# Memory gates formed by rows and turned through DRAM, in a four-layer decoder trunk

## The chip, the core and the metric

One core of a Trainium2 chip runs the whole program. The metric is the device time of one execution in microseconds: before the change 2497.29 us, the median of three runs (2496.13, 2497.29 and 2500.47). TensorE (PE) multiplies, VectorE (DVE) and ScalarE (ACT) work on its results, GpSimd (POOL) here mostly issues DMAs, and SyncE (SP) issues the loads of the weights.

## The reference

Four layers, each with one input projection and one output projection, over 256 tokens of width 2048 in float32. Layers 0 and 3 mix tokens by latent attention, layer 1 by sparse attention, layer 2 by a sliding window; each layer also has four memory heads of width 256. Cut to what matters here:

```python
for i in range(DEPTH):
    h = _rmsnorm(x, norm_in[i])
    self_out, mq, gate = <mixer>(h, w_in, ...)        # h @ w_in, split
    mem_out = _memory_attention(mq, mem_n @ w_mem_kv[i])
    y = jnp.concatenate([self_out, mem_out], axis=-1) * jax.nn.silu(gate)
    x = x + y @ w_out[i]
return _rmsnorm(x, final_norm)
```

The gate has 3072 columns: 2048 for the self heads and 1024 for the memory heads. The norm's factor of each token (`rstd`) is not multiplied into `h` but into each product of it. With z = rstd * product / 2, SiLU of the gate is (tanh(z) + 1) * z.

## The kernel before, in words

**Products.** Each float32 operand is split in two parts, `hi` rounded to the matmul's format (ScalarE) and `lo` = value - `hi` (VectorE), and a product is hi*hi + hi*lo + lo*hi. Weights are loaded by SP into `wr` (five buffers) and split into `wh` and `wl` (`parts_of`, three buffers each). `split_in_order` chains these splits, so that they run in the order in which they are written. There are two forms of product. `rows_by` keeps 128 tokens of the activations in the array and moves 512 weight columns: three matmuls of 512 columns for each 128 rows of the weight (a k-tile) and each of two token tiles; the result has tokens on the partitions. `columns_by` keeps 128 weight columns in the array and moves the tokens' `hi` and `lo` side by side (512 columns) under `wh`, and `hi` alone (256 columns) under `wl`: for a k-tile of 256 weight columns two matmuls of 512 and two of 256 columns; the result has features on the partitions and the tokens along the free axis, in two sums that are added afterwards.

**Layers.** The gate and the output are worked off in six parts of 512 columns, in the order 4, 0, 1, 2, 3, 5: parts 4 and 5 belong to the memory heads, 0 to 3 to the self heads. A part projects its queries, issues its scores and softmax (`memory_attend`, `attend`), forms its gate, and leaves a list `steps`: `parts(0)`, `summed(0)`, `parts(1)`, `summed(1)`. `parts` splits the turned probabilities, `summed` multiplies them with the values (matmuls into `mo` or `o`) and ends in `gated` or `paired`, which multiply the sum with the gate `gT` and split the result into `y`. Then `w_out` multiplies the `y` of the part before (`pending`) with its rows of the output weight, in four chunks of 512 columns, and adds them to `x`. `rows_of_two` makes the first two chunks together.

**Two ways to a gate.** `gated` needs the gate with features on the partitions. Parts 0 to 3 use `gate_by_rows`: product by rows; ScalarE scales each row by its factor (a column of 128 values, `halves`) and takes the tanh; VectorE forms (tanh + 1) * z and transposes it in blocks of 32 x 32; POOL stores each token tile to DRAM and, when both have landed, fetches it back in four DMAs in the turned order. Parts 4 and 5 use `gate`: product by columns in two halves of 256 columns; `total` adds the two sums; VectorE multiplies by `nm.half`, in which the tokens' factors lie along the free axis and are the same on all partitions; tanh and the last step write `gT` in SBUF. `nm.half` is made once for each layer by `spread` (lines 179 to 185): two diagonal matrices, multiplied by ones.

**Order.** Each engine works through its own queue in order. A planner with modelled times sets that order when the program is built, by readiness and written order. `keep_in_program_order` pins an instruction to the written order, and `issue_after` puts one behind another on its engine. `hooks` are lists of functions that a product calls behind the given k-tile, which sets their place in the written order.

**Around the end of a layer.** After part 5's gate (lines 1382 to 1387) come chunks 0 and 1 of the pending part 3, part 5's sums, chunk 2 of the pending part, chunks 0 and 1 of part 5 itself, chunk 3 of the pending part, and chunks 2 and 3 of part 5. In the last layer (lines 1374 to 1381) part 5's own product comes after all four chunks of the pending one. In latent layers the steps of parts 4 and 0 to 3 are called as soon as the part's gate and the pending `w_out` are written (lines 1370 to 1373).

Of the kernel before, what the change touches and what calls it, by code (L numbers as in the profile page):

```python
# [15 lines left out]
P = 128  # L16
S = 256
# [16 lines left out]
def kernel(ctx: ExitStack, tc: tile.TileContext, a: dict, out: bass.AP,  # L34
# [141 lines left out]
            y = y2  # L176


    def spread(dst, cols):
        pr = misc("spr")  # L180
        for t in range(2):
            dg = wk.tile([P, S], F32, name="dg", tag="e", bufs=4)[:, :P]
            nc.vector.tensor_scalar(dg, ident, cols[:, t:t + 1], None, op0=OP.mult)
            nc.tensor.matmul(pr[:, t * P:(t + 1) * P], ones, dg, start=True, stop=True)
        nc.vector.tensor_copy(dst, pr[:, :S])


    def square_sum(col, src):
        junk = tmp("junk")
        return nc.scalar.activation(junk[:, :src.shape[-1]], src, AF.Square, accum_out=col)  # L190
# [166 lines left out]
                f()  # L357
        return acc if apart else whole

    def total(acc):  # L360
        z = wk.tile([P, 2, S], F32, name="z", tag="z", bufs=2)
        copy_act(z, acc[:, :, 1, :])
        nc.vector.tensor_add(z, z, acc[:, :, 0, :])
        return z

    def head_parts(dst, acc):

        z = wk.tile([P, 2, S], F32, name="zl", tag="z", bufs=2)
# [14 lines left out]
    class Norm:  # L383
# [38 lines left out]
        def finish(self):  # L422
            s2 = small("xs2", 2)
            nc.vector.tensor_reduce(s2, self.ss.rearrange("p (t c) -> p t c", t=2), AX.X, OP.add)
            self.rstd = small("xr", 2, bufs=3)
            rsqrt_mean(self.rstd, s2, D)
            self.eighth = small("x8", 2, bufs=3)
            nc.vector.tensor_scalar(self.eighth, self.rstd, 0.125, None, op0=OP.mult)
            half = self.halves = small("xh", 2, bufs=3)
            nc.vector.tensor_scalar(half, self.rstd, 0.5, None, op0=OP.mult)  # L430
            self.half = wk.tile([P, S], F32, name="half", tag="half", bufs=1)
            spread(self.half, half)

        def col(self, which, t):
            return getattr(self, which)[:, t:t + 1]
# [144 lines left out]
            copy_act(dst(i0, i1), f32(tp)[:, :(i1 - i0) * n].rearrange("p (j c) -> p j c", c=n)[:, :, 64 * late:])  # L580


    def gate(nm, w, c0, hooks):
        gT = None
        for h in range(2):
            z = total(columns_by(nm.at, 16, w, 0, (c0 + h * S, S), "g", hooks[h]))
            if gT is None:
                gT = act.tile([P, 4, S], F32, name="gT", tag="gT", bufs=1)
            nc.vector.tensor_mul(z, z, nm.half[:, None, :].to_broadcast([P, 2, S]))
            th = gT[:, 2 * h:2 * h + 2, :]  # L590
            nc.scalar.activation(th, z, AF.Tanh)
            nc.vector.scalar_tensor_tensor(th, th, 1.0, z, op0=OP.add, op1=OP.mult)
        return gT


    def gate_by_rows(nm, w, c0, hooks={}, between={}):
        acc = rows_by(nm.at, 16, w, 0, (c0, 512), "gr", hooks, None, between)
        gT = act.tile([P, 8, 4, 32], F32, name="gTr", tag="gT", bufs=1)
# [16 lines left out]

    def gated(y, o, gT, j):
        yt = wk.tile([P, 512], F32, name="yt", tag="yt", bufs=1)
        if gT.shape[1] == 8:
            nc.vector.tensor_mul(yt.rearrange("p (a t b) -> p a t b", a=2, b=32),
                                 o.rearrange("p (a t b) -> p a t b", a=2, b=32),  # L620
                                 gT[:, :, j:j + 2, :].rearrange("p t a b -> p a t b"))
        else:
            nc.vector.tensor_mul(yt, o, gT[:, j:j + 2, :].rearrange("p a b -> p (a b)"))
        y3 = yt.rearrange("p (a b) -> p a b", a=2)
        split(y[:, 0, j:j + 2, :], y[:, 1, j:j + 2, :], y3)

# [119 lines left out]
    def memory_project(nm, i, w, mq0, g0, part, steps, deferred, loaded=None, begun=None):  # L746
        qT, kT = [], []
        raw, v = loaded or memory_loads(i, part)

        def keys():  # L750
            hi = act.tile([P, 1024], F32R, name="mkh", tag="pq", bufs=PQ)
            tc.keep_in_program_order(copy_act(hi, f32(raw)))
            nc.vector.tensor_sub(raw, f32(raw), f32(hi))
            kT.extend(z.rearrange("p (t m b) -> p t m b", m=4, b=32) for z in (hi[:], raw[:]))
        for h in range(2):
            if part == 0:
                hooks = ({}, {4: [] if begun is not None else steps[:1]})[h]
            elif deferred:
                hooks = ({}, {4: steps[:1], 8: steps[1:2]})[h]
            else:  # L760
                hooks = ({0: steps[:1], 8: steps[1:3]}, {0: steps[3:]})[h]
            if h:
                hooks[8] = hooks.get(8, []) + [keys]
            acc = begun if h == 0 and begun is not None else columns_by(
                nm.at, 16, w, 0, (mq0 + part * 512 + h * 256, 256), "mq", hooks)
            q = act.tile([P, 2, 2, S], F32R, name="mqT", tag="pq", bufs=PQ)
            head_parts(q, acc)
            qT.append(q)
        if begun is not None:
            hooks = {4: steps}, {}  # L770
        elif deferred:
            hooks = {}, {0: steps[2:3], 4: steps[3:]}
        else:
            hooks = {8: [] if part else steps[1:]}, {}
        return (nm, kT, v, qT), lambda: gate(nm, w, g0 + 2048 + part * 512, hooks)

    def memory_attend(nm, kT, v, qT):
        ws = []
# [548 lines left out]
    for i in range(depth):  # L1327
# [22 lines left out]
        for part in (4, 0, 1, 2, 3, 5):  # L1350
# [16 lines left out]
            if part != 5:  # L1367
                if pending is not None:
                    w_out(*pending, False)
                if kind == 0:  # L1370
                    for f in steps:
                        f()
                    steps = []
# [75 lines left out]
```

## Time and profile before

| | us |
|---|---|
| time, median of three runs | 2497.29 |
| time of the profiled execution | 2496.1 |
| its span | 2494.3 |
| TensorE busy | 2483.5 (100%) |
| VectorE busy | 1806.1 (72%) |
| ScalarE busy | 1427.7 (57%) |
| GpSimd busy | 400.8 (16%) |

The span runs from the first to the last instruction. PE is the matmuls; PEld, the loading of the array, overlaps them. A busy TensorE says little, since matmuls overlap each other in the records: the distance of two starts tells what a matmul takes. The tiles of the two gates are `acc_g` (by columns) and `acc_gr` (by rows).

### The profile page before, as it was taken

How to read it: one execution, taken by the hardware profiler on the slowest of the kernel's cores; microseconds unless marked ns; L12 is line 12 of the kernel's file. 1: busy time of each engine (PE TensorE's matmuls, PEld its weight loads, DVE VectorE, ACT ScalarE, POOL GpSimd, SP SyncE). 2: the span in 40 equal slices, each digit the busy share in tenths (PEclk: the TensorE clock that was granted, in tenths of full speed). 3: DMA queues.
4: the chain of work that ended last, by engine and by line, in shares of the span. 5: the costliest groups of instructions: out<-in, count | busy, mean ns of one | idle time of the engine just before them, and what ended most of it. 6: DMA issues, size and time to landing. Idle time of an engine off the chain costs nothing.

```text
span 2494.3 us, 36407 instructions
## 1 busy us (share of the span) xinstructions
PE 2483.5 (100%) x12452; PEld 2109.9 (85%) x12452; DVE 1806.1 (72%) x3061; ACT 1427.7 (57%) x2278; POOL 400.8 (16%) x639
## 2 busy tenths in 40 slices
PE   9999999999999999999999999999999999999998
PEld 7888888888888888888888888888888888888887
DVE  6555655777677676878888775888887677767677
ACT  6444545555555556656666564666665655555554
POOL 1101011211120110112232101212220112012010
PEclk9999999999999999999999999999999999999999
DMA  9888887977877768689999697999978797788774
GB/s 311 279 292 284 283 281 221 260 208 214 220 226 219 217 221 243 193 268 271 264 284 262 197 285 217 283 270 271 270 223 252 232 251 217 198 220 241 239 210 147
DMA packets 462281, 607.59 MB, mean 244 GB/s; under 512 B 79536, under 2 KB 278976, under 8 KB 460944
## 3 DMA queue, kind: packets, MB, share of 16 engines
q1 hardware_dynamic: 420704, 476.92, 63.9%
q0 software_dynamic: 40672, 127.43, 17.3%
q8 instruction: 98, 1.61, 0.3%
q10 hardware_dynamic: 720, 0.93, 0.1%
q14 instruction: 87, 0.71, 0.1%
HBM read 541.49 MB, written 76.25 MB: 248 GB/s over the span
## 4 chain that ended last, share of the span: by engine, by line
PE 98%; DVE 1%; DMA 1%; ACT 0%; SPq 0%; issue 0%; DVEq 0%; ACTq 0%
PE acc_gr L329 5%; PE acc_gr L330 5%; PE acc_gr L328 5%; PE acc_g L352 5%; PE acc_mq L352 4%; PE acc_wo L328 4%; PE acc_wo L329 4%; PE acc_wo L330 4%; PE acc_qn L352 4%; PE acc_wo L243 3%; PE acc_wo L241 3%; PE acc_wo L242 3%; PE acc_q L329 2%; PE acc_q L330 2%; PE acc_q L328 2%; PE acc_mk L329 2%
## 5 line engine op out<-in xcount | busy, mean ns | idle before, releaser
L73 DVE TENSOR_TENSOR wl<-wr,wh 128x1024 fp32r<-128x1024 f32 (+2 forms) x860 | 1028.1, 1197 | 513.3 <-ACT wh L59 506.7
L59 ACT ACTIVATE wh<-wr 128x1024 fp32r<-128x1024 f32 (+2 forms) x860 | 891.3, 1038 | 811.0 <-PE acc_gr L330 96.9
L330 PE MATMUL acc_gr<-wh,xT 128*128 128x512 f32 x512 | 199.7, 390 | 0.0
L329 PE MATMUL acc_gr<-wl,xT 128*128 128x512 f32 x512 | 199.6, 390 | 0.0
L328 PE MATMUL acc_gr<-wh,xT 128*128 128x512 f32 x512 | 199.6, 390 | 0.0
L328 PE MATMUL acc_wo<-wh,y 128*128 128x512 f32 x432 | 168.3, 390 | 0.0
L330 PE MATMUL acc_wo<-wh,y 128*128 128x512 f32 x432 | 168.3, 390 | 0.0
L329 PE MATMUL acc_wo<-wl,y 128*128 128x512 f32 x432 | 168.3, 389 | 0.0
L352 PE MATMUL acc_g<-xT,wh 128*128 128x512 f32 x512 | 162.5, 395 | 0.0
L664 POOL DMA_DIRECT2D pL<-turn x192 | 120.2, 633 | 207.8 <-DMA turn<-T 111.5
L352 PE MATMUL acc_mq<-xT,wh 128*128 128x512 f32 x480 | 152.0, 396 | 0.0
L243 PE MATMUL acc_wo<-wh,y 128*128 128x512 f32 x320 | 124.9, 390 | 0.2 <-DVE y L63 0.2
L241 PE MATMUL acc_wo<-wh,y 128*128 128x512 f32 x320 | 124.9, 390 | 0.0
L242 PE MATMUL acc_wo<-wl,y 128*128 128x512 f32 x320 | 124.8, 390 | 0.0
L1346 DVE TENSOR_TENSOR x<-x,acc_wo 128x1024 f32<-128x1024 f32 x92 | 111.7, 1214 | 13.5 <-PE acc_wo L330 9.5
L352 PE MATMUL acc_qn<-cT,wh 128*128 128x512 f32 x384 | 121.3, 396 | 0.0
L354 PEld LDWEIGHTS acc_g<-xT,wl 128*128 128x128 f32 x512 | 95.6, 188 | 22.2 <-DVE wl L73 0.9
L330 PEld LDWEIGHTS acc_gr<-wh,xT 128*128 128x128 f32 x512 | 96.1, 188 | 19.6
L329 PEld LDWEIGHTS acc_gr<-wl,xT 128*128 128x128 f32 x512 | 96.1, 188 | 18.6
L328 PEld LDWEIGHTS acc_gr<-wh,xT 128*128 128x128 f32 x512 | 96.1, 188 | 18.6
L354 PEld LDWEIGHTS acc_mq<-xT,wl 128*128 128x128 f32 x480 | 89.0, 188 | 19.3
L354 PE MATMUL acc_g<-xT,wl 128*128 128x256 f32 x512 | 102.1, 279 | 0.1
(375 smaller groups left out, 5664.7 us busy)
## 6 DMA issues: line engine op xcount, KB each, us to landing
wr<-in_w_out_dram SPq DMA_DIRECT2D x192, 512.0 KB, 4.9
wr<-in_w_in_a_dram SPq DMA_DIRECT2D x176, 512.0 KB, 4.7
wr<-in_w_mem_kv_dram SPq DMA_DIRECT2D x126, 512.0 KB, 6.3
wr<-in_w_in_b_dram SPq DMA_DIRECT2D x116, 512.0 KB, 4.9
wr<-in_w_in_c_dram SPq DMA_DIRECT2D x104, 512.0 KB, 5.1
wr<-in_w_uq_dram SPq DMA_DIRECT2D x192, 128.0 KB, 3.5
turn<-T POOLq DMA_DIRECT2D x40, 384.0 KB, 5.1
tab<-flat POOLq DMA_DIRECT2D x8, 1536.0 KB, 11.5
```

The lines of the kernel that those rows point to most:

```text
L59: return nc.scalar.activation(o, i, AF.Copy, scale=scale)
L73: two = nc.vector.tensor_sub(lo, src, f32(hi))
L241: nc.tensor.matmul(accs[c][:, t], xh, wh[:, at], start=first, stop=False)
L242: nc.tensor.matmul(accs[c][:, t], xh, wl[:, at], start=False, stop=False)
L243: nc.tensor.matmul(accs[c][:, t], xl, wh[:, at], start=False, stop=last)
L328: nc.tensor.matmul(acc[:, t, :n], xh, wh[:, at], start=first, stop=False)
L329: nc.tensor.matmul(acc[:, t, :n], xh, wl[:, at], start=False, stop=False)
L330: nc.tensor.matmul(acc[:, t, :n], xl, wh[:, at], start=False, stop=last)
L352: nc.tensor.matmul(acc[j], wh[:, at[j]], q[:, :, kt % 4, :], start=first, stop=False)
L354: nc.tensor.matmul(acc[j][:, 0, :], wl[:, at[j]], q[:, 0, kt % 4, :], start=False, stop=last)
L664: nc.gpsimd.dma_start(f32(self.raw)[j * 32:(j + 1) * 32, :].rearrange("p (i r) -> p i r", r=r), bass.AP(tensor=d.tensor, offset=d.offset + ...
L1346: nc.vector.tensor_add(xs, xs, acc)
```

## The change

`gate`, `total` and `spread` go, and with them `nm.half`. The memory parts call `gate_by_rows`, and `gated` keeps the one form that reads its layout. The hooks of the gate's product are renumbered from two half products of four k-tiles a step to one product of two k-tiles a step, at about the same share of the work. In latent layers the steps of part 4 are no longer called at once: they are handed to `project(0)`, whose first product, of the rotary queries, takes them as hooks behind its k-tiles 0, 4 and 8.

```diff
-    def spread(dst, cols):
-        pr = misc("spr")
-        for t in range(2):
-            dg = wk.tile([P, S], F32, name="dg", tag="e", bufs=4)[:, :P]
-            nc.vector.tensor_scalar(dg, ident, cols[:, t:t + 1], None, op0=OP.mult)
-            nc.tensor.matmul(pr[:, t * P:(t + 1) * P], ones, dg, start=True, stop=True)
-        nc.vector.tensor_copy(dst, pr[:, :S])
...
-    def total(acc):
-        z = wk.tile([P, 2, S], F32, name="z", tag="z", bufs=2)
-        copy_act(z, acc[:, :, 1, :])
-        nc.vector.tensor_add(z, z, acc[:, :, 0, :])
-        return z
...
             nc.vector.tensor_scalar(half, self.rstd, 0.5, None, op0=OP.mult)
-            self.half = wk.tile([P, S], F32, name="half", tag="half", bufs=1)
-            spread(self.half, half)
...
-    def gate(nm, w, c0, hooks):
-        gT = None
-        for h in range(2):
-            z = total(columns_by(nm.at, 16, w, 0, (c0 + h * S, S), "g", hooks[h]))
-            if gT is None:
-                gT = act.tile([P, 4, S], F32, name="gT", tag="gT", bufs=1)
-            nc.vector.tensor_mul(z, z, nm.half[:, None, :].to_broadcast([P, 2, S]))
-            th = gT[:, 2 * h:2 * h + 2, :]
-            nc.scalar.activation(th, z, AF.Tanh)
-            nc.vector.scalar_tensor_tensor(th, th, 1.0, z, op0=OP.add, op1=OP.mult)
-        return gT
...
     def gated(y, o, gT, j):
         yt = wk.tile([P, 512], F32, name="yt", tag="yt", bufs=1)
-        if gT.shape[1] == 8:
-            nc.vector.tensor_mul(yt.rearrange("p (a t b) -> p a t b", a=2, b=32),
-                                 o.rearrange("p (a t b) -> p a t b", a=2, b=32),
-                                 gT[:, :, j:j + 2, :].rearrange("p t a b -> p a t b"))
-        else:
-            nc.vector.tensor_mul(yt, o, gT[:, j:j + 2, :].rearrange("p a b -> p (a b)"))
+        nc.vector.tensor_mul(yt.rearrange("p (a t b) -> p a t b", a=2, b=32),
+                             o.rearrange("p (a t b) -> p a t b", a=2, b=32),
+                             gT[:, :, j:j + 2, :].rearrange("p t a b -> p a t b"))
...
         if begun is not None:
-            hooks = {4: steps}, {}
+            hooks = {2: steps}
         elif deferred:
-            hooks = {}, {0: steps[2:3], 4: steps[3:]}
+            hooks = {8: steps[2:3], 10: steps[3:]}
         else:
-            hooks = {8: [] if part else steps[1:]}, {}
-        return (nm, kT, v, qT), lambda: gate(nm, w, g0 + 2048 + part * 512, hooks)
+            hooks = {4: [] if part else steps[1:]}
+        return (nm, kT, v, qT), lambda: gate_by_rows(nm, w, g0 + 2048 + part * 512, hooks)
...
-                if kind == 0:
+                if kind == 0 and part != 4:
                     for f in steps:
                         f()
                     steps = []
```

## Rows read from the trace of the kernel before

**Rows 1.** The page: span, and the chain that ended last by engine.
```profile
span 2494.3 us, 36407 instructions
...
PE 98%; DVE 1%; DMA 1%; ACT 0%; SPq 0%; issue 0%; DVEq 0%; ACTq 0%
```

**Rows 2.** Waits of TensorE: who waited, for whom, total us, times, longest.
```profile
PE msp L789 <- ACT mkh L59: 0.5, 1, 0.5
```

**Rows 3.** Timeline of TensorE, layer 0, part 5's gate by columns: start, us, instruction.
```profile
876.56 0.63 PE L352 MATMUL acc_g<-xT,wh 128*128 128x512 f32 x2
...
885.62 0.63 PE L352 MATMUL acc_g<-xT,wh 128*128 128x512 f32 x2
```

**Rows 4.** Timeline of TensorE, layer 0, part 0's gate by rows.
```profile
555.98 0.39 PE L328 MATMUL acc_gr<-wh,xT 128*128 128x512 f32 x1
...
567.99 0.39 PE L330 MATMUL acc_gr<-wh,xT 128*128 128x512 f32 x1
```

**Rows 5.** Timeline of TensorE, the spread at the start of layer 1.
```profile
956.61 0.61 PE L184 MATMUL spr<-dg,ones 128*128 128x128 f32 x4
956.98 0.48 PE L261 MATMUL acc_iq<-wh,xT 128*128 128x512 f32 x1
957.29 0.39 PE L259 MATMUL acc_kv<-wh,xT 128*128 128x512 f32 x1
```

**Rows 6.** Timeline of TensorE, layer 1, part 4's gate.
```profile
1052.94 0.63 PE L352 MATMUL acc_g<-xT,wh 128*128 128x512 f32 x2
1053.56 0.51 PE L354 MATMUL acc_g<-xT,wl 128*128 128x256 f32 x2
...
1055.98 0.63 PE L352 MATMUL acc_g<-xT,wh 128*128 128x512 f32 x2
1056.67 0.51 PE L354 MATMUL acc_g<-xT,wl 128*128 128x256 f32 x2
```

**Rows 7.** By tile: first all stores of gTt, then all fetches of gTr.
```profile
DMA to landing us min/median/max: 2.4/3.9/6.3
...
DMA to landing us min/median/max: 2.9/4.9/7.3
```

**Rows 8.** Timeline of POOL behind part 0's gate of layer 0.
```profile
577.12 0.56 POOL L608 DMA_DIRECT2D turned<-gTt  x1 [1.81 <-DVE gTt L544]
581.89 2.34 POOL L610 DMA_DIRECT2D gTr<-turned  x4 [4.22 <-issue]
```

**Rows 9.** Timelines of VectorE and ScalarE behind part 5's gate of layer 0.
```profile
903.86 0.69 DVE L623 TENSOR_TENSOR yt<-mo,gT 128x512 f32<-128x512 f32 x1
905.25 0.69 DVE L63 TENSOR_TENSOR y<-yt,y 128x512 fp32r<-128x512 f32 x1 [0.70 <-ACT y L59]
...
904.58 0.63 ACT L59 ACTIVATE y<-yt 128x512 fp32r<-128x512 f32 x1 [1.93 <-DVE yt L623]
```

**Rows 10.** Timeline of TensorE there: the gate's end, part 5's sums, its product.
```profile
890.27 0.39 PE L354 MATMUL acc_g<-xT,wl 128*128 128x256 f32 x2
...
901.39 0.28 PE L812 MATMUL mo<-pH,mvr 128*128 128x256 f32 x1
...
909.69 0.39 PE L328 MATMUL acc_wo<-wh,y 128*128 128x512 f32 x1
```

**Rows 11.** Windows of 20 us behind gates: busy us of each engine, clock, DMA share, GB/s.
```profile
568.00:588.00 20.00, 20.00 (x90) 16.60 (x89) 14.98 (x16) 10.89 (x13) 5.95 (x10) 1.00 0.93 246
890.00:910.00 20.00, 20.00 (x102) 17.03 (x101) 15.12 (x18) 9.63 (x13) 0.00 (x0) 1.00 0.51 171
1400.00:1420.00 20.00, 20.00 (x102) 17.03 (x102) 16.01 (x19) 10.06 (x13) 0.00 (x0) 1.00 0.47 161
1857.00:1877.00 20.00, 19.80 (x101) 16.52 (x100) 16.09 (x19) 10.60 (x14) 2.34 (x4) 1.00 0.50 167
```

**Rows 12.** Timeline of VectorE behind part 4's gate of layer 0, which ends at 495.52.
```profile
507.98 0.69 DVE L623 TENSOR_TENSOR yt<-mo,gT 128x512 f32<-128x512 f32 x1 [1.58 <-PE mo L812]
```

**Rows 13.** Timeline of TensorE at the start of the program.
```profile
5.13 0.80 PE L328 MATMUL acc_mv<-wh,mT 128*128 128x512 f32 x1
```

## The prediction, on record before the changed kernel was run

> **What bounds the kernel now.** I read the page first. TensorE is busy for 2483.5 of 2494.3 us and the chain that ended last lies on it for 98% [rows 1]; its longest wait inside the layers for another engine's work is 0.5 us, once, for a memory key [rows 2]. So nothing that the change takes from VectorE, ScalarE or the DMA queues is worth anything by itself. It counts in two ways only: fewer microseconds of matmul issue, and new waits in front of a matmul. "Busy" hides the first, since matmuls overlap: the reader should look at starts. In the timeline of TensorE the by-columns gate starts a new pair of 512-column matmuls at 876.56 and the thirteenth pair after it at 885.62 [rows 3]: 9.06/13 = 0.697 us for one k-tile of 256 gate columns (two matmuls of 512 columns and two of 256). The gate by rows has 53 matmuls of 512 columns from the start at 555.98 to the one at 567.99 [rows 4]: 0.2266 us each, 0.680 us for three, the same 1536 columns. The same work, in three instructions where there were four.
>
> **The change part by part.**
>
> *The eight memory gates by rows (parts 4 and 5 of four layers).* 8 gates x 16 k-tiles x 2 halves = 256 groups, each 0.697 - 0.680 = 0.017 us cheaper: 4.3 us off TensorE.
>
> *The spread of the row factor is gone.* In each layer four short matmuls start at 956.61, the next product starts at 956.98, and the one after it at 957.29 [rows 5]: 0.37 us, and 0.31 - 0.23 = 0.08 us for the odd product behind them. 4 layers x 0.45 = 1.8 us.
>
> *VectorE and ScalarE at the gate.* Gone are, twice per gate, an add from PSUM and a multiply of 128x512; new are, twice per gate, a 128x512 transpose and, in place of the unscaled copy, a scaled one. I cost that at nothing: TensorE's splits are made up to three tiles ahead. One place shows what this cover is worth. In the part 4 gate of the sparse layer, behind its selection, VectorE was late with a `wl`, and starts that should be 0.47 apart are 0.62 (1052.94 to 1053.56) and 0.69 (1055.98 to 1056.67), with 0.11 more behind each [rows 6]: 0.6 us. The add and the multiply of the first half stood among those splits; by rows nothing of the gate falls there. I take the 0.6 us as saved; its bounds are 0 and 0.6.
>
> Gains together: 4.3 + 1.8 + 0.6 = 6.7 us.
>
> *The new way of the gate through DRAM.* This is the cost. I count from the start of the last gate matmul, "+t". The gate by rows of the latent layers is the nearest row, since it too is followed by an output product of two chunks: its last matmul starts at 567.99 [rows 4], the second store to DRAM is issued at 577.12, the four fetches from 581.89 on, together 2.34 us of issuing [rows 8], that is +9.1, +13.9 and the last at +15.7. A store lands 2.4 to 6.3 us after its issue, median 3.9, a fetch 2.9 to 7.3, median 4.9 [rows 7]. From the second store to the first fetch are 4.8 us here; 0.5 of them I count, as an estimate, to POOL itself behind the landing. With the medians the gate is there at 9.1 + 3.9 + 0.5 + 1.75 + 4.9 = +20.2; with the shortest at 9.1 + 2.4 + 0.5 + 1.75 + 2.9 = +16.7; with the longest at +25. Until now it never left the core's SBUF.
>
> *Who waits for it: part 5 of the first three layers.* After the gate come 48 matmuls of the pending output product, 24 `mo` matmuls, 24 more of chunk 2, and then the product that reads part 5's own `y`. In the trace: gate end 890.27 + 0.12, `mo` from 901.39, first `y` product at 909.69 [rows 10], so +19.3. Nothing can go before it: the split weights go in written order through three buffers, and chunk 3 of the pending part stands behind the two chunks that need `y`. From the gate's arrival to `y` are one multiply, one copy and one subtraction: 903.86, 904.58, 905.25 + 0.69 = 905.94 [rows 9], 2.1 us, say 2.2 with the semaphore. So the gate must be there by +17.1, and its arrival is +16.7 at best, +20.2 by the medians. Which end? The medians come from stretches where the DMA engines are 0.93 busy; after the part 5 gates they are 0.51, 0.47 and 0.50 busy and POOL issues next to nothing [rows 11]. I take +17.5, near the short end: a wait of 0.4 us, and 0.3 us for the second half of `y`, which has one `yt` buffer and follows by 2.1 us at least, where 12 matmuls of 0.23 give 2.7. So 0.7 a layer, 2.1 us in all; bounds 0 and 3 x 7.9.
>
> By the Trainium skill (DMA: Bandwidth & Descriptors, "Anatomy of one DMA — SWDGE (gpsimd) path") such a DMA takes about 2.0 us plus its bytes over 436 GB/s, an estimate of 2.6 us for a store of 256 KB and 2.3 us for a fetch of 128 KB. That gives +16.3, no wait, and the time of rival 1. The trace agrees only with the shortest store; none of its 64 fetches landed in under 2.9 us [rows 7].
>
> *The latent layers' part 4.* Its sums are now spread over the rotary query product instead of being called at once; the planner already let them run there (`yt` at 507.98, +12.5 after the gate [rows 12]), so the 24 matmuls move within TensorE's queue and cost the same. The copies and subtractions of `parts` and the pinned order move with them. On POOL the gate's six DMAs come ahead of the rotary stores; a fetch that waits for its store holds POOL from about +9 to +16, and the rotary rows behind it are ready only when a product of 12 x 1.36 us is over, at +16.4: nothing waits. VectorE is the risk: if `yt` still stands at +12.5 in its queue, it stands still until about +20 with weight splits behind it. I expect the planner to place it later and take 0.6 us for both latent layers, the last layer's part 5 (first use of `y` about 5.5 us later than in the others) and the two part 4 gates of the other layers together; bounds 0 and 13 us (rival 3).
>
> *Elsewhere.* Weights of these gates come as 2 KB rows instead of 1 KB rows; no wait of TensorE for them stands in the trace, so nothing.
>
> **Sum.** -6.7 + 2.1 + 0.6 = -4.0 us. The profiled execution took 2496.1 us, 1.2 below the median of 2497.3: 2492.1 against it, and 2493.3 against the median.
>
> **The rivals.**
>
> 1. *No wait at all.* The gate is there by +17.1 everywhere. For it: half-idle DMA engines [rows 11] and the shortest landings [rows 7]. Against it: four fetches of one gate must all be short. -6.7: 2490.6.
>
> 2. *The wait for the gate eats the gain (slower than before).* Place: the first product on part 5's `y` in the first three layers. With median landings `y` is there at +20.2 + 2.2 = +22.4 against +19.3: 3.1 us in each, 9.3 in all, -6.7 + 9.3 = +2.6: 2499.9. It decides from 2.2 us a layer on, an arrival at +19.3. For it: the medians, over 16 gates. Against it: the quieter DMA engines. With arrivals at +22, as under the load of the latent projections, it is 4.9 a layer: 2505.
>
> 3. *VectorE stands still for the gate in the latents' part 4.* A `yt` left at +12.5 blocks for some 8 us. Splits are three tiles ahead, a tile is 12 matmuls, 2.7 us, and the next split takes about 2.3, so some 3 us are covered and 5 lost, in two to three places: +10 to +15, less 4.6 gained net elsewhere: about 2502 to 2507. Against it: instructions are ordered by a planner that knows of the DMA.
>
> 4. *The clock falls in the waits.* At the start the first 512-column matmul is 0.80 long where later ones are 0.39 [rows 13, 4]. If each of three waits of 3 us (rival 2) brought back that state for some 3 us of work, each would lose 1.5 more: 2499.9 + 4.5 = 2504. The Trainium skill (TensorE: Matmul & The Clock Gate, "HAM oscillation — how this bites in real kernels") says that idle gaps of TensorE between bursts bring the clock back to half. Nothing in the middle of this trace tests it.
>
> **How the numbers follow.** A measurement of this kernel tells a change from none at about 0.2%, 5 us: faster is below 2492.3, slower above 2502.3. Chances: forecast (2490.5 to 2496.5) 0.52, rival 1 0.22, rival 2 0.16, rival 3 0.06, rival 4 0.04. Faster takes rival 1 and two fifths of the forecast: 0.43. Slower takes a third of rival 2 and most of rivals 3 and 4: 0.13. The rest, 0.44, is within 0.2%. The range, 2489 to 2502, holds rival 1, the forecast and rival 2 at its medians; the likeliest case alone is 2490.5 to 2496.5.
>
> **What would show it.** Right: all eight gates in groups of three at 0.68 us; no `spr` matmuls; the gate's last fetch landing at +17 to +18 in part 5; a gap of TensorE under 1 us in front of the first product on part 5's `y` in layers 0 to 2; no `wl` wait in the sparse layer's part 4 gate. Wrong: such gaps of 2 us and more (rival 2), a VectorE wait on the fetches in the latents' part 4 with a `wl` late behind it (rival 3), a granted clock under 1.0 in the middle (rival 4), or waits in places that I have not named.

## The result and the profile after

The changed kernel takes 2520.71 us (median of 6 runs, 2516.99 to 2526.66) where the kernel before took 2496.71 (6 runs on the same chip): ratio 1.0096, interval [1.0082, 1.011]. Predicted were 2493.3, and 2502 at most: it is 24.0 us slower where 4 us of gain were forecast, and no part of the range reached it.

The page of after answers to [rows 1]. TensorE is still busy for nearly the whole span, so busy time does not tell where 23.2 us of span went. The shares of the chain that ended last do not tell it either: followed back from the end, this chain stops at a store of a gate at 1884 us, so its shares add up to some 26% and can't be held against the 98% of before. Where it stops is telling, though: on the way of part 5's gate in layer 2, from the fetches to the first product that needs `y` (second block: start, us, what).

```profile
span 2517.5 us, 35923 instructions
...
PE 2487.4 (99%) x12180; PEld 2099.2 (83%) x12180; DVE 1788.8 (71%) x3033; ACT 1428.9 (57%) x2278; POOL 430.1 (17%) x687
...
PE 23%; issue 1%; DMA 1%; DVE 1%; POOL 0%; ACT 0%; DVEq 0%; POOLq 0%
```

```profile
1888.44 1.37 POOL gTr L580 x3
...
1890.20 7.18 DMA gTr<-turned
...
1898.96 0.80 PE acc_wo L319
```

The waits of TensorE tell more (who waited for whom: total us, times, longest). Before, the longest wait of this kind was 0.5 us, once [rows 2].

```profile
PE acc_wo L319 <- ACT y L59: 12.5, 3, 5.3
PE acc_gr L320 <- DVE wl L73: 3.4, 4, 2.1
```

The three waits for `y` are part 5's product in layers 0 to 2. In layer 0 the timeline of TensorE shows the gap, and something more behind it (start, us, instruction): the matmuls after the gap start 0.6, 0.42 and 0.59 us apart, and are 0.63 to 0.79 long where they were 0.39.

```profile
908.43 0.39 PE L321 MATMUL acc_wo<-wh,y 128*128 128x512 f32 x1
913.99 0.79 PE L319 MATMUL acc_wo<-wh,y 128*128 128x512 f32 x1 [5.18 <-ACT y L59]
914.59 0.63 PE L320 MATMUL acc_wo<-wl,y 128*128 128x512 f32 x1
915.01 0.63 PE L319 MATMUL acc_wo<-wh,y 128*128 128x512 f32 x1
915.60 0.79 PE L320 MATMUL acc_wo<-wl,y 128*128 128x512 f32 x1
```

The same stretch by windows (busy us of each engine, granted clock, DMA share, GB/s): the granted clock is 1.00 up to the gap, 0.50 for the five microseconds after it (1.2 in place of 2.4 GHz), and back at 0.97 behind that.

```profile
889.00:908.00 19.00, 19.00 (x97) 16.18 (x96) 12.75 (x15) 9.60 (x12) 4.39 (x8) 1.00 0.75 230
908.00:914.00 6.00, 0.82 (x5) 0.36 (x3) 1.87 (x3) 1.69 (x2) 0.00 (x0) 0.87 0.57 149
914.00:919.00 5.00, 5.00 (x11) 3.33 (x12) 3.52 (x5) 0.63 (x1) 0.00 (x0) 0.50 0.33 108
919.00:924.00 5.00, 5.00 (x23) 4.09 (x22) 1.56 (x2) 2.12 (x2) 0.00 (x0) 0.97 0.03 9
```

I summed, over all neighbouring matmuls behind the first 20 us of the program, how much later the second starts than the steady pace of its shape (0.227 us for 512 columns). The kernel before has some 8.1 us of such excess, this one 35.9: +27.8. Less the 6.1 us that the gates' matmuls and the spread gave back, this is 21.7 of the 23.2 us of span. By place: part 5 of layers 0, 1 and 2 has 8.2, 8.1 and 3.9 us (gaps of 5.3, 5.5 and 2.2, the rest the pace behind them), of the last layer 2.1; part 4 of layers 1 and 2 some 5.5, and 2.5 more in the parts after it in layer 2.

Why `y` is late is on POOL (layer 0, part 5; the last gate matmul starts at 889.24) and in the view of the tile (last line: from issue to landing, shortest, median, longest, of the four fetches).

```profile
895.81 0.58 POOL L578 DMA_DIRECT2D turned<-gTt  x1 [5.92 <-DVE gTt L527]
898.35 0.56 POOL L578 DMA_DIRECT2D turned<-gTt  x1 [1.96 <-DVE gTt L527]
904.27 2.36 POOL L580 DMA_DIRECT2D gTr<-turned  x4 [5.36 <-issue]
```

```profile
DMA to landing us min/median/max: 6.0/6.4/6.7
```

The second store takes 5.2 us, the fetches 6.0 to 6.7: the gate is there at +23.2 (from the start of the last gate matmul, as in the prediction). VectorE waits for it, with other work behind it: `yt` stands 4.1 us, then come an addition to `x` and a weight split, and only then the `lo` part of `y`. The first product needs the `hi` part alone, which ScalarE copies out of `yt`: it starts 1.5 us behind the landing, at 913.99.

```profile
912.59 0.69 DVE L588 TENSOR_TENSOR yt<-mo,gTr 128x512 f32<-128x512 f32 x1 [4.13 <-DMA gTr<-turned]
913.19 1.21 DVE L1313 TENSOR_TENSOR x<-x,acc_wo 128x1024 f32<-128x1024 f32 x1
914.32 1.22 DVE L73 TENSOR_TENSOR wl<-wr,wh 128x1024 fp32r<-128x1024 f32 x1
915.46 0.68 DVE L63 TENSOR_TENSOR y<-yt,y 128x512 fp32r<-128x512 f32 x1
```

In part 4 of layers 1 and 2 nothing on TensorE waits for `y` soon, but VectorE stands at `yt` all the same, for 5.2 and 7.6 us, and the weight splits behind it are late for the next gate product.

```profile
1090.96 0.69 DVE L588 TENSOR_TENSOR yt<-mo,gTr 128x512 f32<-128x512 f32 x1 [5.16 <-DMA gTr<-turned]
...
1555.84 0.69 DVE L588 TENSOR_TENSOR yt<-mo,gTr 128x512 f32<-128x512 f32 x1 [7.55 <-DMA gTr<-turned]
1556.45 1.22 DVE L73 TENSOR_TENSOR wl<-wr,wh 128x1024 fp32r<-128x1024 f32 x1
...
1557.71 0.50 PE L320 MATMUL acc_gr<-wl,xT 128*128 128x512 f32 x1 [2.06 <-DVE wl L73]
```

### The profile page after: what moved, and what is told of

Read it like the earlier page. It is cut to its first block, busy times and chain, and to the rows that moved or that the text cites. A ratio compares the mean times of both kernels' runs of the same rounds, so it can differ in the third digit from the quotient of the medians.

```text
span 2517.5 us, 35923 instructions
## 1 busy us (share of the span) xinstructions
PE 2487.4 (99%) x12180; PEld 2099.2 (83%) x12180; DVE 1788.8 (71%) x3033; ACT 1428.9 (57%) x2278; POOL 430.1 (17%) x687
## 5 line engine op out<-in xcount | busy, mean ns | idle before, releaser
L320 PE MATMUL acc_gr<-wl,xT 128*128 128x512 f32 x768 | 300.0, 391 | 3.4 <-DVE wl L73 3.4
L321 PE MATMUL acc_gr<-wh,xT 128*128 128x512 f32 x768 | 299.6, 390 | 0.0
L319 PE MATMUL acc_gr<-wh,xT 128*128 128x512 f32 x768 | 299.4, 390 | 0.0
L319 PE MATMUL acc_wo<-wh,y 128*128 128x512 f32 x432 | 171.6, 397 | 13.5 <-ACT y L59 12.5
L320 PEld LDWEIGHTS acc_gr<-wl,xT 128*128 128x128 f32 x768 | 144.2, 188 | 33.3 <-DVE wl L73 5.5
L321 PEld LDWEIGHTS acc_gr<-wh,xT 128*128 128x128 f32 x768 | 144.2, 188 | 29.3
L319 PEld LDWEIGHTS acc_gr<-wh,xT 128*128 128x128 f32 x768 | 144.2, 188 | 27.9
L319 PEld LDWEIGHTS acc_wo<-wh,y 128*128 128x128 f32 x432 | 82.7, 191 | 32.8 <-ACT y L59 13.7
L626 POOL DMA_DIRECT2D turn<-T x56 | 42.9, 766 | 370.3 <-DVE T L620 313.5
L345 PEld LDWEIGHTS acc_mq<-xT,wl 128*128 128x128 f32 x480 | 89.0, 188 | 19.3
L320 PE MATMUL acc_mv<-wl,mT 128*128 128x512 f32 x256 | 100.2, 391 | 0.7 <-DVE wl L73 0.7
```

The costliest lines, as they stand in the source:

```text
L319: nc.tensor.matmul(acc[:, t, :n], xh, wh[:, at], start=first, stop=False)
L320: nc.tensor.matmul(acc[:, t, :n], xh, wl[:, at], start=False, stop=False)
L321: nc.tensor.matmul(acc[:, t, :n], xl, wh[:, at], start=False, stop=last)
L345: nc.tensor.matmul(acc[j][:, 0, :], wl[:, at[j]], q[:, 0, kt % 4, :], start=False, stop=last)
```

## The experiments

The theory was: the gate lands too late for part 5's `y`, the wait lowers TensorE's clock, and VectorE standing at `yt` costs the rest in part 4. Ratios are to the kernel before, run on the same chip. The waits named are of the profiled runs.

**Which part costs it.** Two kernels undo half of the change each:

```diff
-return (nm, kT, v, qT), lambda: gate_by_rows(nm, w, g0 + 2048 + part * 512, hooks)
+# p5_columns (p4_columns has the two the other way round)
+return (nm, kT, v, qT), lambda: (gate(nm, w, g0 + 2048 + part * 512, hooks) if part else
+                                 gate_by_rows(nm, w, g0 + 2048, rhooks))
```

> Undoes part 5 of the change alone: part 4's gate by token rows and through DRAM, part 5's by columns as before (with the row factors spread as before). Theory A (the loss is part 5's y, late because its gate comes back from DRAM some 22 to 23 us after the last gate matmul, with a lower clock after each wait: 20.1 us in layers 0 to 2 and 2.1 in the last): of the 24.0 us lost those 22 go, less half of the gain of the gates' matmuls (2.1) and of the spread (1.8) that go with them: 2520.7 - 22 + 4 = 2503, between 2499 and 2507. Rival B (TensorE's order or pace of the row products costs it everywhere): half of the loss stays, about 2509. Rival C (the waits of part 4, VectorE standing at yt, are most of it): 2515 or more.

> Undoes part 4 of the change alone: part 4's gate by columns, part 5's by token rows and through DRAM. Theory A: only the stalls of part 4 in layers 1 and 2 go (7 to 8 us of them on TensorE), and 2.1 us of the gates' gain and 1.8 of the spread with them: 2516 to 2518. Rival B (order or pace everywhere): about 2509. Rival C (part 4's waits are most of it): 2503 or less.

Part 5 by columns: 2502.86 us, 1.0019 [1.001, 1.0028]. Part 4 by columns: 2514.53 us, 1.0069 [1.0055, 1.0083]. So of the 0.96% that the change costs 0.77 go with part 5's new way and 0.27 with part 4's, each net of the matmuls that it saves. Both kernels also bring the spread back, some 1.8 us (0.07%), so the two shares add up to more than the whole. Theory A had the first right and somewhat less for the second (2516 to 2518). B and C are out.

**The clock.** 48 idle matmuls fill the gaps (in the trace each is two of 0.11 us, so that they take 4.4, 4.4 and 1.8 us in layers 0, 1 and 2, twice what the forecast took):

```diff
+def fill():
+    spare = misc("spare")
+    with tc.issue_after(last_mm[0].ins):
+        for n_ in range((20, 20, 8)[i]):
+            one = nc.tensor.matmul(spare[:, :P], ones, ones, start=True, stop=True)
+    return one.ins
-w_out(part, y, True, range(2))
+w_out(part, y, True, range(1), {0: [fill]})
+w_out(part, y, True, range(1, 2))
```

> The changed kernel with 20, 20 and 8 matmuls of ones by ones (128 columns, some 0.11 us each, nothing reads them) put on TensorE between chunk 2 of part 3's product and part 5's y product of layers 0, 1 and 2, where it stands for 5.3, 5.5 and 2.2 us. Theory A' (the slow matmuls behind the gap, 0.43 us start to start until some 5 us after it, are the lower clock that the gap brought): the gap stays, partly filled, the matmuls behind it run at 0.227 and 7.1 us go: 2513 to 2515. Rival F (they are slow because the second half of y comes 2.2 us after the first and VectorE's casts behind it): nothing goes, 2520 to 2521, and the pace behind the gap is as in the changed kernel.

1.0075 [1.0058, 1.0092], 2516.86 us: some 5 us better than the changed kernel by the ratios (0.0021 x 2497), between the two forecasts. The two intervals overlap a little, so the trace has to show what the matmuls did. The windows show that the clock stays:

```profile
907.00:914.00 7.00, 6.96 (x51) 6.16 (x50) 3.73 (x4) 1.85 (x3) 0.00 (x0) 1.00 0.56 165
914.00:919.00 5.00, 4.39 (x18) 3.43 (x19) 2.59 (x5) 1.69 (x2) 0.00 (x0) 1.00 0.32 105
```

Part 5's product still began at 913.01 only, 4.6 us after its predecessor, but 1.3 us are lost behind that in place of 2.8, those to a weight split and the late `lo` part of `y`. In layers 1 and 2 it is 1.3 in place of 2.6, and 0.1 in place of 1.7. So the clock is a cause of its own, of about 1.5 us per gap; rival F accounts for the remaining 1.3 in layers 0 and 1. In this profiled run, the fastest of the four, the gates also landed 1.0 to 1.2 us earlier, which shortened the gaps themselves, apart from the clock.

**Why the gate is late.** First the weights of chunks 1 to 3 of part 3's product were not loaded, then those of part 5's product neither; a third kernel read the gate back in whole rows.

```diff
+if k0 in kept_wr:                    # reuse; reuse_more: k0 % 4, and for part 5 too
+    return kept_wr[k0], n
 wr = wp.tile([P, ST * 512], F32, name="wr", tag="wr", bufs=WR)
...
-bass.AP(tensor=d.tensor, offset=d.offset + j * P, ap=[[512, 32], [32 * 512, 8], [1, P]])
+bass.AP(tensor=d.tensor, offset=d.offset + j * 32 * 1024, ap=[[1024, 32], [1, 1024]])   # fetch_whole
```

> The changed kernel, but chunks 1 to 3 of part 3's product at the end of layers 0 to 2 reuse the weights that chunk 0 has loaded, so that no weights are loaded for them in the 20 us in which the gate goes through DRAM (this leaves 9 of 12 weight loads out, and computes those chunks with chunk 0's weights). Theory A (the gate lands late because the weights' loads share the DMA engines): the stores land some 2.4 us and the fetches some 3 us after their issue, the gate lands at +17 to +18 and the waits of 5.3, 5.5 and 2.2 us fall to under 1.5 each. Rival G (store and fetch take that long by themselves): landing stays at +21 or more and the waits stay.

> The changed kernel with the four fetches of each memory gate and recent gate reading whole rows of 4 KB per partition in place of eight pieces of 512 bytes; the same bytes, but other elements than the gate's (so the gates' values are permuted). Theory P (the size of the pieces sets the fetch): a fetch lands about 2.5 to 3 us after its issue (now 6 to 6.7 in part 5 of layer 0), the gate at +18 to +19, and the waits of 5.3, 5.5 and 2.2 us fall to under 2. Rival Q (bytes and the weights' loads beside them set it): 5 us or more, landing at +21 or later, the waits as they were.

> The changed kernel, but in layers 0 to 2 chunks 1 to 3 of part 3's product and all four of part 5's reuse the weights loaded for chunk 0 of part 3's (so 7 of 8 chunks' weight loads are left out, and those chunks are computed with the wrong weights): hardly any weights are loaded while the gate goes through DRAM. Theory A (weights' loads beside the gate make it late): stores 4.6 to 5.5 us from first issue to last landing, fetches about 5 us from first issue to last landing (8.2, 8.8 and 8.9 in the changed kernel), gate at +17 to +18.5, waits under 1.5 us in layers 0 and 1, none in layer 2. Rival G (four fetches of one gate take 7 to 9 us by themselves): gate at +20 or later, waits of 2.5 us and more in layers 0 and 1.

*reuse* (2512.69 us, one run) was inconclusive. The gate came at +21.4, +22.3 and +18.6 in layers 0 to 2, and waits of 3.3, 4.3 and 0 us stayed. The stores were quicker (2.3 and 3.4 us in layer 0), the fetches took 3.5 to 6.4 us; but part 5's own weights had moved up, and 155 to 175 KB/us of weights ran beside the fetches, more than in the changed kernel (139 to 143). What I wrote as the test of contention did not remove it.

*fetch_whole* (2517.45 us, one run): the size of the pieces is not the main thing; the 2.5 to 3 us of theory P did not come. Fetches of part 5 in layer 0:

```profile
DMA to landing us min/median/max: 3.6/4.8/5.8
```

The gate came at +20.9 and gaps of 3.0, 3.6 and 1.2 us remained. Even this is not the pieces alone: the first two fetches now need the first store only and were issued 3 us earlier. What the pieces themselves cost is not told apart.

*reuse_more*, whose products at the end of the layers use wrong weights, settled it. Its rows, by windows of 20 us behind two of the gates as in [rows 11], and for the fetches in layer 0:

```profile
889.00:909.00 20.00, 20.00 (x101) 17.04 (x100) 14.44 (x16) 10.11 (x13) 3.49 (x6) 1.00 0.18 57
1408.00:1428.00 20.00, 20.00 (x101) 16.80 (x100) 15.85 (x18) 8.68 (x11) 3.48 (x6) 1.00 0.17 53
```

```profile
DMA to landing us min/median/max: 3.0/3.0/3.1
```

No weight byte moved between the first store and the last landing in those three places. The stores took 2.3 us each, the fetches 2.8 to 4.0, and the gates were there at +16.9, +17.0 and +17.3. No gap is left in part 5 of layers 0 to 2; the run took 2502.27 us. The other memory gates of the same run, their weights loaded as ever, still came at +19.6 to +26.8. So rival G is out: the weights' loads beside it make the gate 4.6 to 6.3 us late. What the loads and the gate's DMAs compete for was not told apart.

**VectorE standing at the gate.** y_last moves part 5's `y` product behind all of part 3's; y_late also puts the steps that form `y` ahead of chunk 3 in place of chunk 2. y_last_hooks, y_late and p5_columns_hooks hook part 4's first steps later, p4_later later still.

```diff
-w_out(*pending, False, range(2, 3), {0: [steps[0], steps[2], steps[1], steps[3]]})
-w_out(part, y, True, range(2))
-w_out(*pending, False, range(3, 4))
-w_out(part, y, True, range(2, 4))
+w_out(*pending, False, range(2, 3))                                                  # y_late
+w_out(*pending, False, range(3, 4), {0: [steps[0], steps[2], steps[1], steps[3]]})
+w_out(part, y, True)
...
-acc = rows_by(..., "q", {8: steps[:1], 10: steps[1:2]})
+acc = rows_by(..., "q", {8: steps[:1], 10: steps[1:2]} if g else {10: steps[:1], 14: steps[1:2]})   # _hooks
+acc = rows_by(..., "q", {8: steps[:1], 10: steps[1:2]} if g else {14: steps[:1]})                   # p4_later,
+gate_by_rows(..., hooks, {14: steps[2:]} if g else {2: steps[1:2], 14: steps[2:]})                  # both lines
```

> The changed kernel with one thing moved: in layers 0 to 2 the two first chunks of part 5's y product run after chunk 3 of part 3's product and not ahead of it, so y is needed 5.5 us later (24.8 us after the last gate matmul and not 19.3). Nothing is added or left out. Theory A: the waits of 5.3, 5.5 and 2.2 us shrink to under 0.5 each, and with them goes the lower clock after them (7.1 us): 2520.7 - 20 = 2501, between 2499 and 2505. Rival D (the gate's landing goes back by as much, because the later weights press on it): the waits stay, 2515 or more.

> The kernel with the later y, and the first half of the attention's deferred steps in part 4 hooked two and four k-steps pairs later (10 and 14 in place of 8 and 10 of the first group's product), so that VectorE meets yt later. Theory A: the waits behind VectorE standing at yt in part 4 of layers 1 and 2 (stood 5.2 and 7.6 us, some 7 us on TensorE) shrink too by half or more: 2494 to 2499, near the kernel before's 2496.7 or below it. Rival E (steps moved later only move the same wait to the wl casts of the next product): no better than the kernel with the later y alone, 2501 or more.

y_last: 2512.92 us, 1.0059 [1.0045, 1.0072]; only some 9 us of the 20 went. The gap of 5.3 us is gone, but the layer still lost 3.1 us in two places, and the timelines of VectorE and TensorE show why: `yt` stands as long as before, now ahead of a split that the `y` product itself needs.

```profile
913.06 0.69 DVE L588 TENSOR_TENSOR yt<-mo,gTr 128x512 f32<-128x512 f32 x1 [4.04 <-DMA gTr<-turned]
913.67 1.21 DVE L1313 TENSOR_TENSOR x<-x,acc_wo 128x1024 f32<-128x1024 f32 x1
914.79 1.22 DVE L73 TENSOR_TENSOR wl<-wr,wh 128x1024 fp32r<-128x1024 f32 x1
...
916.07 0.50 PE L320 MATMUL acc_wo<-wl,y 128*128 128x512 f32 x1 [0.58 <-DVE wl L73]
```

y_last_hooks: 2512.04 us, 1.0057 [1.0044, 1.007]. In part 4 the gaps in front of the next gate product shrank (2.8 to 1.2 us in layer 1, 3.8 to none in layer 2), but the total hardly moved, since others came in layer 2; rival E is not excluded by this run.

> The changed kernel with part 5's y product of layers 0 to 2 run last, as in the run with the later y, and in addition the steps that form y stand ahead of chunk 3 and not of chunk 2, and part 4's first steps are hooked at 10 and 14. Theory A'' (with y due at +24.8 what was left was VectorE standing 4 us at yt with the x add and a wl cast behind it): VectorE meets yt some 5 us later, the waits of 3.1, 5.8 and 4.8 us left in part 5 of the three layers fall to about 1 us each, 10 go: 2500 to 2504. Rival (y itself is too late for +24.8): 2509 to 2512, as with the later y alone.

> Part 5's gate by columns as before, part 4's by rows, and part 4's first deferred steps hooked at 10 and 14 of the next product. Theory A: of the 6.8 us in which TensorE waits in part 4 of layers 1 and 2, 3 to 5 go: 2498 to 2500, level with the kernel before.

> Part 5's gate by columns, part 4's by rows; part 4's steps moved on in layers 1 and 2: the first one hooked at 14 of the next query product, its sums (with yt) at 2 of the gate product after it. If VectorE standing at yt is what is left in part 4, the 3.5 us that TensorE still waits there (1.1, 1.4 and 1.1 us in layer 1) go: 2495 to 2497, 1.5 to 3 us under the kernel before. Rival: the later sums only move the wait to that gate product's casts: 2499 or more.

y_late: 2505.53 us, 1.0031 [1.0021, 1.004], a little over the forecast of theory A'' and some 6.5 us less than y_last_hooks, from which it differs only in that the steps stand one chunk (24 matmuls, 5.4 us) later in VectorE's queue. Now the `x` addition and the split are ahead of `yt`, and the `y` product begins 0.41 after its predecessor, though the gate still lands at +23.5:

```profile
912.96 0.69 DVE L588 TENSOR_TENSOR yt<-mo,gTr 128x512 f32<-128x512 f32 x1 [4.52 <-DMA gTr<-turned]
914.36 0.69 DVE L63 TENSOR_TENSOR y<-yt,y 128x512 fp32r<-128x512 f32 x1 [0.70 <-ACT y L59]
...
913.97 0.39 PE L321 MATMUL acc_wo<-wh,y 128*128 128x512 f32 x1
914.38 0.50 PE L319 MATMUL acc_wo<-wh,y 128*128 128x512 f32 x1
```

`yt` stands 4.5 us here too. What such a wait costs TensorE hangs on when `y` is due and on what is queued behind `yt`. By the starts of the profiled runs, part 5 of layers 0 to 2 with the first products of the next layer loses 20.1 us in the changed kernel, 13.8 in y_last (its slowest run), 9.5 in y_last_hooks and 5.3 in y_late. Of the 1.7 us that are left in layer 0 of y_late, 0.2 stand in front of the `y` product and 1.1 at a split in the next layer.

p5_columns_hooks: 2499.07 us, 1.0003 [0.9995, 1.0012]; p4_later: 2498.08 us, 0.9999 [0.999, 1.0008]. With the later hooks the waits of part 4 shrink and then go, and the time is level with the kernel before. The forecast gain of 1.5 to 3 us for p4_later did not show; the interval (-2.5 to +2 us) can't exclude the small end of it. TensorE's waits for a split in the gate products of that kernel:

```profile
PE acc_gr L329 <- DVE wl L73: 0.2, 1, 0.2
```

**The gate earlier.** The other way to give it time: part 5's gate product ahead of that part's two query products (gate_first), or between them (gate_mid, with y_late's order), its way back issued behind them.

```diff
+sent = gate_sent(nm, w, g0 + 2048 + part * 512, ...)   # product and stores; sent() allocates and fetches
 for h in range(2):
     ...columns_by(nm.at, 16, w, 0, (mq0 + part * 512 + h * 256, 256), "mq", hooks)
-return (nm, kT, v, qT), lambda: gate_by_rows(nm, w, g0 + 2048 + part * 512, hooks)
+return (nm, kT, v, qT), sent
```

> The changed kernel with part 5's gate product put ahead of that part's two query products, and its way back from DRAM issued behind them: the same instructions in another order, so that the gate has 14.6 us more before y is needed (+34 and not +19.3). Theory A (the loss is the gate's way through DRAM against y's due time): part 5's waits and the lower clock after them go in all four layers (22 us), the waits of part 4 in layers 1 and 2 stay (6 to 7 us): 2497 to 2501. Rival H (the attention's softmax, now with only the w_out product to cover it, is late in place of the gate): a new wait on TensorE's mo of 3 to 5 us per layer, 2505 to 2515.

> The same order, and the first half of part 4's deferred steps hooked at 10 and 14 of the next product and not at 8 and 10. Theory A: the waits of part 4 shrink by 3 to 6 us as well: 2492 to 2497, at or under the kernel before's 2496.7 to 2498. Rival H: as without the later hooks, less 2 to 4.

> As the kernel with the late y, and in layers 0 to 2 part 5's gate product stands between that part's two query products (7.3 us earlier, y due at some +32), and its way back from DRAM is issued behind them. Theory A: gate and y are there in time, and the second query product's softmax has 22 us of matmuls to cover it where it had 11 with the gate ahead of both: no wait over 1 us in part 5, 2493 to 2498. Rival H (the softmax, about 15 us from its last score to mo, is late again): waits at mo of 2 to 4 us with a lower clock behind, 2505 to 2520.

All three are far slower: 2542.08 us (1.0172 [1.0157, 1.0187]), 2537.10 (1.0153 [1.0138, 1.0168]) and 2532.12 (1.0129 [1.0113, 1.0144]). Rival H was right, and dearer than I had it. In gate_first TensorE waits for the probabilities:

```profile
PE mo L789 <- ACT pH L59: 22.5, 7, 4.7
```

They too go through DRAM. In gate_mid the second half's are stored at 902.98, behind the moved query product, and fetched from 906.86 on; TensorE, at the second half's sums from 907.3 on, stands still for 7.2 us (POOL, then TensorE):

```profile
902.98 0.77 POOL L632 DMA_DIRECT2D turn<-T  x1 [8.42 <-DVE T L626]
906.86 2.60 POOL L637 DMA_DIRECT2D pL<-turn  x4 [3.11 <-PE acc_wo L321]
...
914.51 0.58 PE L793 MATMUL mo<-pH,mvr 128*128 128x256 f32 x1 [7.15 <-ACT pH L59]
```

The slot behind the query products is worth at least as much to the probabilities as to the gate: what was taken from the one wait came back in another. The clock adds to it: over the 14 us from 904, 1430 and 1904 in gate_first the granted clock is 0.51, 0.51 and 0.52. My 15 us from the last score to the sums were a distance in the old order, not the time that the way takes: here the last score matmuls start before 894.9 and the probabilities are split at 914.5.

**The best of it, by rows.** y_late with p4_later's hooks, and part 5 of the last layer by columns:

> All parts by rows but part 5 of the last layer; part 5's y product last, the steps that form y ahead of chunk 3, and part 4's steps moved on as in the kernel beside it. Of the 7 us that the kernel with the late y is over the kernel before, some 3 go with part 4 and 2 with the last layer's part 5: 2499 to 2502. Rival, as beside: 2504 or more.

2502.67 us, 1.002 [1.0011, 1.0029]: a little over the forecast. Some 18 of the 24 us are back, by order and by the last layer's old way, but this kernel is still 5 us slower than the kernel before, and no version was measurably faster.

## Why the prediction was wrong

*Gates by rows, spread (-4.3, -1.8).* Right, as far as the rows go: in part 5 of layer 0 the gate runs from 874.51 to 888.79 in 21 groups, 0.680 us each, and no `spr` matmul is left. The sum of 6.1 us was not measured by itself.

```profile
874.51 0.39 PE L319 MATMUL acc_gr<-wh,xT 128*128 128x512 f32 x1
...
888.79 0.39 PE L319 MATMUL acc_gr<-wh,xT 128*128 128x512 f32 x1
```

*The `wl` waits of the sparse layer's part 4 (-0.6).* Not saved: that gate product still loses 0.5 us for a split, and the product behind it 0.8.

*The way through DRAM: this step failed.* The prediction had the chain of steps right (second store at +9.1; `y` due at +19.3, measured +19.4 in layers 0 and 1) and bounded the landing between +16.7 and +25. The 2.2 us from the landing to `y` were 1.5, since the first product waits for the `hi` part alone. Of that span the prediction took +17.5, "near the short end", because the DMA engines are 0.51, 0.47 and 0.50 busy there [rows 11]. Measured: +23.2, +23.3 and +21.9. In layer 0 that is 9.1 + 5.2 (the second store) + 0.7 + 1.8 + 6.4 (the last fetch); the two DMA terms, 2.4 and 2.9 at the short end, are what was mis-sized. A share of 0.5 over 20 us was read as a half idle path. It is a mean of bursts and pauses, as single microseconds of the kernel before show:

```profile
903.00:904.00 1.00, 1.00 (x11) 1.00 (x10) 1.00 (x2) 0.00 (x0) 0.00 (x0) 1.00 0.92 344
904.00:905.00 1.00, 1.00 (x8) 0.87 (x7) 0.55 (x1) 0.42 (x1) 0.00 (x0) 1.00 0.17 55
```

In the changed kernel the loads went on while the gate was under way: from the first store's issue to the last one's landing weights moved at 153 to 171 KB/us, beside the fetches at 139 to 143. With these loads gone the same DMAs gave +17 (reuse_more), so the short end was the price of an empty path. And the share of before leaves out the gate's own 1 MB (0.5 stored, 0.5 fetched): with it the same stretches are 0.77, 0.69 and 0.80 busy.

```profile
889.00:909.00 20.00, 19.82 (x99) 16.53 (x97) 13.21 (x15) 9.74 (x13) 4.39 (x8) 1.00 0.77 230
1408.00:1428.00 20.00, 20.00 (x100) 16.69 (x98) 13.50 (x15) 9.59 (x12) 4.87 (x8) 1.00 0.69 203
1875.00:1895.00 20.00, 20.00 (x104) 17.06 (x103) 13.20 (x16) 9.06 (x12) 6.09 (x10) 1.00 0.80 226
```

The medians of [rows 7], from gates that the same kernel sent under the same loads, would have been the nearer row, and even they (+20.2) were 2 to 3 us short. The term of 2.1 us measured 20.1 (22.2 with the last layer).

*Rivals 2 and 4 together are what happened.* Rival 2 had the place, the mechanism and the slope right; its worse case of +22 was 4.9 us a layer, measured 5.3, 5.5 and 2.2. Layer 2 waits less for two reasons: its gate lands 1.3 us earlier, and `y` is due at +21.3 there, since sums of part 3 (`o`, 1.9 us) now run between the gate and the pending product; the prediction had +19.3 for all three. Rival 4 was put at 1.5 us per gap and a chance of 0.04: behind the gaps 2.8, 2.6 and 1.7 us were lost, and the fill run puts about 1.5 of the 2.8 down to the clock. That its 1.5 agrees is partly luck: it was read from a long matmul at the start of the program, where the profile shows a granted clock of 1.00 (0 to 6 us), and for some 3 us of work, where the windows behind the first gap show 5 at 0.50. The two rivals are not independent: here the lower clock came behind each of the three waits, so 0.04 should have been most of rival 2's chance. By the Trainium skill (TensorE: Matmul & The Clock Gate, "HAM oscillation — how this bites in real kernels") gaps between bursts bring half clock back; these rows agree, 0.50 granted behind a gap of 5.3 us.

*VectorE standing still (0.6 us, rival 3).* The mechanism is real, the place was not the latents' part 4. There the planner moved `yt` from +12.5 [rows 12] to 517.25, +22.5 after the gate's end at 494.78, and TensorE lost nothing, as forecast; the latent sums' move into the next product was not tested by itself. It struck in part 4 of layers 1 and 2, which the 0.6 lumped in without a row of their own: 5.5 us, and 2.5 more behind them whose cause is not shown.

*Numbers.* -6.1 gained of -6.7; +20.1 for +2.1 and some +10 for +0.6; some 2.4 us of small stalls that the kernel before had elsewhere are gone: 21.7 of the 23.2 us of span, 1.5 not placed. The range's upper end, 2502, stood on rival 2 at its medians; with its longest landings (3 x 7.9, the prediction's own bound) and the clock it would have reached 2519.

## What to carry to other kernels

A value that leaves the core's SBUF on the way to a matmul has to be budgeted with the landings measured under the loads that will run beside it; a DMA share averaged over a product says nothing of the microseconds in which it moves. When such a value may be late, let it be due later and put the waiting VectorE instruction behind what other products need from that queue: with some 4 us of standing in each case, part 5 of layer 0 lost 8.2 us in one order and 1.7 in another. Before moving a product up to buy time, ask whose slot it takes: here the probabilities needed the same one.

## What the runs showed of the hardware

Beside weights' loads of 140 to 170 KB/us a store of 256 KB took 5.2 to 5.3 us in part 5 of layer 0 and a fetch of 128 KB 6.0 to 6.7; with none beside them (part 5 of layers 0 to 2 of reuse_more) 2.3 and 2.8 to 4.0. The Trainium skill's figures (DMA: Bandwidth & Descriptors, "Anatomy of one DMA — SWDGE (gpsimd) path") gave estimates of 2.6 and 2.3 us. The measured store of the quiet path agrees within 0.3 and the fetch is longer; on the busy path the store took twice its estimate and the fetch 2.6 to 2.9 times.

A gap of 2.2 us (part 5 of layer 2) was followed by a granted clock of 0.58, one of 2.1 us in part 4 of the same layer by 1.00:

```profile
1899.00:1903.00 4.00, 4.00 (x11) 3.15 (x12) 3.90 (x5) 2.44 (x3) 0.00 (x0) 0.58 0.05 12
...
1558.00:1562.00 4.00, 4.00 (x19) 3.26 (x19) 4.00 (x8) 3.31 (x5) 1.09 (x2) 1.00 0.64 169
```

What tells these two apart was not tried.
